# Loads and products of the RWKV-7 scan in another order: keys, queries, values

## The chip, the cores and the metric

The kernel runs on one core of a Trainium2 chip. The metric is the device time of one launch in microseconds. The engines are PE (matmul), PEld (its weight load), DVE, ACT, POOL and SP; SP issues nearly all transfers. A step's matmuls in float32 appear in the trace as two rows for each product of the code.

## What is computed

Two layers over 512 latent and 256 context tokens of width 1024. Layer 0 is a hybrid of attention and a gated linear recurrence. Layer 1 is a bidirectional RWKV-7 mixer, and its scan is the stage of the change:

```python
def wkv_scan(r, w, kk, bvec, k, v, s0, reverse):
    def step(s, inp):
        r_t, w_t, kk_t, b_t, k_t, v_t = inp
        sk = jnp.einsum('bhvk,bhk->bhv', s, kk_t)
        s = s * w_t[:, :, None, :] - sk[..., None] * b_t[:, :, None, :] + v_t[..., None] * k_t[:, :, None, :]
        return s, jnp.einsum('bhvk,bhk->bhv', s, r_t)
    ...
    s_fin, y = lax.scan(step, s0, xs, reverse=reverse)

def rwkv7_mixer(...):
    ...
    for d, rev in enumerate((False, True)):
        s_c, y_c = wkv_scan(rc, dc[d][0], kkc, dc[d][1], dc[d][2], vc, s0, rev)
        _, y_l = wkv_scan(rl, dl[d][0], kkl, dl[d][1], dl[d][2], vl, s_c, rev)
```

## The kernel before

The scan is done in chunks of 64 tokens, both directions at once: `order` (line 1049) lists 12 steps, four of the context and then eight of the latents, each with a forward and a backward chunk. A step works on eight pairs of heads, `kt` 0 to 7, of 128 channels.

Stages ahead of the scan write to DRAM, chunk by chunk: `kbd` (keys and removal vectors with their decay), `qld` and `qcd` (queries of latents and context), `vd` (values), `ld` (the triangles to be inverted). The scan loads them again.

`tm_feed(i)` (line 1052) prepares step `i`, and is a generator that yields between its parts. Its first part loads: the keys KB (two tiles, for pairs 0 to 3 and 4 to 7, each loaded in two halves), the queries QZ (two halves, into one of two standing tiles), the values W (two halves). Then come four groups of products of QZ and KB, each for two pairs, masked by DVE into G (line 1082), and then two groups that turn KB by PE with the identity (line 1096), which ACT copies into KT. `tm_step(i, kt)` (line 1159) is the scan of one pair: products of G and W, of the inverted triangle XT and rh, the update of W by DVE, products of KT and W into the new state S, and for latents the outputs from W, G, S and QZ. It has 20 products for each pair in a latent step.

`tm_scan` (line 1276) runs both together: after each `tm_step(i, kt)` it takes one part of `tm_feed(i + 1)`. So in the text the loads of step `i + 1` stand behind pair 0 of step `i`, the four groups of products behind pairs 1 to 4, the two groups of turns behind pairs 5 and 6. Between them stand the loads and the inversion of a triangle (`tm_invert`, at pair 0 of every second step), the two parts of `tm_below` (pairs 2 and 4), and from step 9 on the group norm of finished chunks (`tm_post`, at pair 2), which loads bo.

Buffers set what may run when. KB has two tiles, W two, QZ two standing ones: the queries of step `i + 1` go where step `i - 1` read its own. The products, the turns, `tm_below` and the z of `tm_post` share the two PSUM tiles mm2.

The text's order is not the order of the queues. The program is written under `tile.TileContext(nc, schedule_with_timeline_sim=True)` (line 1522): a planner lays out each engine's queue in advance, taking at each moment what its plan holds to be ready, and of several ready ones the one that stands first in the text. On the chip each queue then runs in the order laid out.

Of the kernel before, what the change touches and what calls it, by code (L numbers as in the profile page):

```python
# [7 lines left out]
F32 = mybir.dt.float32  # L8
# [7 lines left out]
P = 128  # L16
D = 1024
KT = 8
# [16 lines left out]
class Net:  # L35
# [457 lines left out]
    def recurrence(self, i, ps, gw, m):  # L493
# [3 lines left out]
        rgv = lambda n, i: self.rgv[:, RGV[n], i:i + 1]  # L497
        W = 2 + NL + 3 + NC + 1
        xp = self.sb([P, W], F32, "rgxp", 1)
        for z0, z1 in ((0, 2), (2 + NL, 5 + NL), (W - 1, W)):  # L500
            nc.gpsimd.memset(xp[:, z0:z1], 0.0)
# [442 lines left out]
    def tm_prep(self, kt, lw):  # L944
# [49 lines left out]
        for d in range(2):  # L994
# [4 lines left out]
            else:  # L999
                (nc.vector if kt == KT - 1 else nc.gpsimd).tensor_mul(X[:, 1], X[:, 1], k)  # L1000
                ek, eq, er = E[1][:, :, 0:64], E[0][:, :, 1:65], E[0][:, :, 0:64]
            nc.gpsimd.tensor_copy(self.dec0[:, kt, d], E[1][:, :, 64])
            KB = self.sb([P, 12, 128], F32, "KB", 3)
            nc.vector.tensor_mul(KB.rearrange("p c (b i) -> p b c i", b=2), X.rearrange("p b (c i) -> p b c i", i=64),
                                 ek.unsqueeze(1).to_broadcast([P, 2, 12, 64]))
            nc.sync.dma_start(self.kbd[d, kt], KB)
            ql, qc = self.sb([P, 8, 128], F32, "ql", 3), self.sb([P, 4, 64], F32, "qc", 3)
# [4 lines left out]
            nc.sync.dma_start(self.qcd[d, kt], qc)  # L1012
            KBs.append(KB)
            qs.append((ql, qc))
# [34 lines left out]
    order = [(c, 19 - c) for c in range(8, 12)] + [(c, 7 - c) for c in range(8)]  # L1049
    half = staticmethod(lambda n: slice(64 * n, 64 * n + 64))  # L1050

    def tm_feed(self, i, KB=None, W=None):

        nc, half = self.nc, self.half
        f = self.feeds[i] = {}
        cs = self.order[i]
        lat = cs[0] < 8
        m = 128 if lat else 64
        KB = KB or [self.sb([P, 4, 2, 128], F32, "KB", 2) for _ in range(2)]
        W = f["W"] = W or self.sb([P, KT, 2, 2, 64], F32, "W", 2)  # L1060
        QZ = f["QZ"] = self.QZ[i % 2]
        by = lambda z: z.rearrange("k (n p) m -> p (k n) m", n=2)
        flat = lambda z: z.rearrange("p k n m -> p (k n) m")
        for d in range(2):
            h = half(1 - d)
            for g in range(2):
                nc.sync.dma_start(flat(KB[g][h]), by(self.kbd[d, 4 * g:4 * g + 4, :, cs[d]]))
            nc.sync.dma_start(flat(QZ[h, :, :, d, 0:m]), by(self.qld[d, :, :, cs[d]] if lat else self.qcd[d, :, :, cs[d] - 8]))
        for d in range(2):
            v = self.vd[64 * cs[d]:64 * cs[d] + 64].rearrange("t (k n v) -> t k n v", n=2, v=64)  # L1070
            nc.sync.dma_start(W[half(d), :, d], v)
        f["G"], f["KT"] = [], []
        yield
        for g in range(4):
            ps = self.mm2()
            for j in range(2):
                for n in range(2):
                    x = 2 * m * (2 * j + n)
                    self.mm(ps[:, x:x + 2 * m], KB[g // 2][:, 2 * (g % 2) + j, n], QZ[:, 2 * g + j, n, :, 0:m], True, True)
            G = self.sb([P, 2, 2, 2, m], F32, "G", 8)  # L1080
            f["G"].append(G)
            nc.vector.tensor_mul(G.rearrange("p k n d t -> p (k n) d t"),  # L1082
                                 ps[:, :8 * m].rearrange("p (k d t) -> p k d t", d=2, t=m),
                                 self.gmask[:, :, 0:m].unsqueeze(1).to_broadcast([P, 4, 2, m]))
            if i:

                for d in range(2):
                    h = half(1 - d)
                    nc.scalar.activation(G[h, :, :, d, 0:64], QZ[h, 2 * g:2 * g + 2, :, d, 0:64], AF.Copy)
            yield  # L1090
        for g in range(2):
            ps = self.mm2()
            for j in range(4):
                for n in range(2):
                    x = 256 * j + 128 * n
                    nc.tensor.transpose(ps[:, x:x + 128], KB[g][:, j, n], self.ident)  # L1096
            T = self.sb([P, 4, 2, 128], F32, "KT", 3, pool=self.gp)
            nc.scalar.activation(T, ps.rearrange("p (k n x) -> p k n x", k=4, n=2), AF.Copy)
            f["KT"].append(T)
            yield  # L1100

    def tm_invert(self, j):
# [56 lines left out]
    def tm_step(self, i, kt):  # L1159
# [4 lines left out]
        g, j = kt // 4, kt % 4  # L1164
        W = f["W"][:, kt]
        XT = self.XT[i // 2][:, i % 2]
        Q = f["QZ"][:, kt]
        G = f["G"][kt // 2][:, kt % 2]
# [107 lines left out]
    def tm_scan(self):  # L1276
        nc, a, half = self.nc, self.a, self.half
        self.gmask = self.sb([P, 2, 128], F32, "gmask")
        nc.sync.dma_start(self.gmask, a["gmask"])
        self.umask = self.sb([P, 2], I32, "umask")  # L1280
        nc.sync.dma_start(self.umask, a["umask"])

        qz = lambda j: self.sb([P, KT, 2, 2, 128], F32, "QZ%d" % j)
        q = qz(0)
        ahead = [self.sb([P, 4, 2, 128], F32, "KB", 2) for _ in range(2)], self.sb([P, KT, 2, 2, 64], F32, "W", 2)
        self.QZ = [q, qz(1)]
        for j, z in enumerate(self.QZ):
            for d in range(2):
                nc.gpsimd.memset(z[half(d), :, :, d], 0.0)  # L1289
        self.feeds, self.S, self.Sd = {}, [None, None], [None, None]  # L1290
        n, below = len(self.order), iter(())
        for _ in self.tm_feed(0, *ahead):
            pass
        for i in range(n):
            feed = self.tm_feed(i + 1) if i + 1 < n else iter(())
            for kt in range(KT):
                self.tm_step(i, kt)
                next(feed, None)
                if i % 2 == 0 and kt == 0 and 0 <= i < n - 4:
                    self.tm_invert(i // 2 + 2)  # L1300
                if i % 2 == 1 and kt == 2 and i + 1 < n:
                    below = self.tm_below(i // 2 + 1)
                if (i % 2 == 1 and kt in (2, 4) or i % 2 == 0 and kt in (2, 4)):
                    next(below, None)
                if i == 1 and kt < 2:
                    src = a["gg"].rearrange("o (k n v) -> o k n v", n=2, v=64)[:, :, kt]
                    nc.sync.dma_start(self.gg[half(kt)], src.to_broadcast([64, KT, 64]))
                if i >= 9 and kt == 2:
                    self.tm_post(i - 5)
                if i == n - 2 and kt == 4:  # L1310
                    self.out1_ahead()
# [216 lines left out]
```

## Time and profile before

| | |
|---|---|
| median of 3 runs | 2261.44 us (2256.51 to 2264.19) |
| profiled execution | 2269.31 us |
| its span | 2267.5 us |
| mean granted clock of PE | 0.942 |
| PE busy | 2023.4 us, 89% |
| DVE busy | 1145.4 us, 51% |
| ACT busy | 869.6 us, 38% |
| POOL busy | 519.6 us, 23% |

The rows below come from the profiled execution. Times count from the start of its span. The scan lies between 1466 and 1820 us. A tile's name before `<-` is what an instruction writes, the names after it are what it reads: `mm<-QZ,KB` are the products, `mm<-ident,KB` the turns, `sc<-...` the scan of the pairs.

### The profile page before, as it was taken

How to read it: one execution, taken by the hardware profiler on the slowest of the kernel's cores; microseconds unless marked ns; L12 is line 12 of the kernel's file. 1: busy time of each engine (PE TensorE's matmuls, PEld its weight loads, DVE VectorE, ACT ScalarE, POOL GpSimd, SP SyncE). 2: the span in 40 equal slices, each digit the busy share in tenths (PEclk: the TensorE clock that was granted, in tenths of full speed). 3: DMA queues.
4: the chain of work that ended last, by engine and by line, in shares of the span. 5: the costliest groups of instructions: out<-in, count | busy, mean ns of one | idle time of the engine just before them, and what ended most of it. 6: DMA issues, size and time to landing. Idle time of an engine off the chain costs nothing. (4 is left out here: it accounts for less than half of the span.)

```text
span 2267.5 us, 37320 instructions
## 1 busy us (share of the span) xinstructions
PE 2023.4 (89%) x15710; PEld 1619.3 (71%) x15710; DVE 1145.4 (51%) x1835; ACT 869.6 (38%) x1333; POOL 519.6 (23%) x530
## 2 busy tenths in 40 slices
PE   5888889999999999997987769779787778999999
PEld 3666547778888888875765449667676666888887
DVE  4556664342222222328647997648575684333333
ACT  3664454231121221317744543346454432232321
POOL 0122331010010100105004983661500220110110
PEclk8999999999999999998998778889898999999999
DMA  7324441123333122212224659396644440222222
GB/s 282 119 86 136 143 164 41 37 94 119 124 129 113 56 64 67 98 42 79 93 88 148 236 223 214 71 143 102 113 91 80 76 140 19 93 93 93 93 93 93
DMA packets 231944, 248.93 MB, mean 110 GB/s; under 512 B 52448, under 2 KB 209504, under 8 KB 225376
## 3 DMA queue, kind: packets, MB, share of 16 engines
q1 hardware_dynamic: 229728, 241.30, 36.8%
q0 software_dynamic: 896, 3.15, 0.4%
q8 instruction: 123, 2.02, 0.4%
q10 hardware_dynamic: 1152, 2.10, 0.2%
q14 instruction: 45, 0.37, 0.1%
HBM read 200.82 MB, written 41.94 MB: 107 GB/s over the span
## 5 line engine op out<-in xcount | busy, mean ns | idle before, releaser
L264 ACT ACTIVATE whi<-wst 128x1024 fp32r<-128x1024 f32 x160 | 169.2, 1059 | 587.3 <-PE mm L47 567.0
L47 PE MATMUL mm<-hhi,whi 128*128 128x512 f32 (+1 forms) x992 | 346.8, 356 | 16.2 <-ACT hhi L250 6.7
L47 PE MATMUL mm<-hlo,whi 128*128 128x512 f32 (+1 forms) x992 | 352.0, 356 | 3.6 <-DVE hlo L251 3.4
L47 PE MATMUL mm<-hhi,wlo 128*128 128x512 f32 (+1 forms) x992 | 349.6, 353 | 0.0
L265 DVE TENSOR_TENSOR wlo<-wst,whi 128x1024 fp32r<-128x1024 f32 x160 | 199.9, 1251 | 255.2 <-ACT whi L264 252.4
L345 POOL TENSOR_TENSOR mp<-mr 128x768 f32<-128x768 f32 (+1 forms) x64 | 109.9, 1719 | 848.1 <-ACT mr L344 848.1
L47 PE MATMUL mm<-ahi,wlo 128*128 128x512 f32 (+1 forms) x704 | 252.9, 359 | 0.0
L47 PE MATMUL mm<-ahi,whi 128*128 128x512 f32 (+1 forms) x704 | 252.9, 360 | 0.0
L47 PE MATMUL mm<-alo,whi 128*128 128x512 f32 (+1 forms) x704 | 252.5, 359 | 0.0
L300 DVE SCALAR_TENSOR_TENSOR Xt<-mm,mod,Xt 128x512 f32<-128x512 f32 (+1 forms) x112 | 70.6, 653 | 336.8 <-PE mm L47 336.6
L47 PEld LDWEIGHTS mm<-hhi,whi 128*128 128x128 f32 x992 | 187.8, 191 | 55.2 <-ACT hhi L250 8.7
L47 PEld LDWEIGHTS mm<-hlo,whi 128*128 128x128 f32 x992 | 188.9, 190 | 32.1 <-DVE hlo L251 6.6
L47 PEld LDWEIGHTS mm<-hhi,wlo 128*128 128x128 f32 x992 | 188.4, 190 | 28.3 <-issue 0.8
L47 PEld LDWEIGHTS mm<-ahi,whi 128*128 128x128 f32 x704 | 132.2, 188 | 28.1 <-issue 6.7
L47 PEld LDWEIGHTS mm<-ahi,wlo 128*128 128x128 f32 x704 | 132.5, 188 | 22.0 <-DVE wlo L265 1.1
L47 PEld LDWEIGHTS mm<-alo,whi 128*128 128x128 f32 x704 | 132.4, 188 | 21.9
L47 PE MATMUL mm<-QZ,KB 128*128 128x256 f32 (+1 forms) x384 | 96.4, 408 | 48.1 <-DMA QZ<-qlr 20.3
L47 PEld LDWEIGHTS mm<-QZ,KB 128*128 128x128 f32 x384 | 74.1, 227 | 60.3 <-issue 26.3
L347 DVE TENSOR_TENSOR alo<-mp,ahi 128x768 fp32r<-128x768 f32 (+1 forms) x64 | 54.9, 858 | 113.1 <-ACT ahi L346 113.0
L1082 DVE TENSOR_TENSOR G<-mm,gmask 128x1024 f32<-128x1024 f32 (+1 forms) x48 | 50.2, 1047 | 88.1 <-PE mm L47 87.8
L346 ACT ACTIVATE ahi<-mp 128x768 fp32r<-128x768 f32 (+1 forms) x64 | 47.3, 739 | 110.3 <-POOL mp L345 110.3
L47 PE MATMUL sc<-W,G 128*64 128x64 f32 (+1 forms) x1280 | 67.8, 233 | 12.8 <-DVE S L1194 10.3
(462 smaller groups left out, 4207.7 us busy)
## 6 DMA issues: line engine op xcount, KB each, us to landing
wst<-in_mlp_w_dram SPq DMA_DIRECT2D x64, 1024.0 KB, 5.4
wst<-in_ada_w_dram SPq DMA_DIRECT2D x48, 1024.0 KB, 6.4
kbr<-KB SPq DMA_DIRECT2D x16, 768.0 KB, 4.5
KB<-kbr SPq DMA_DIRECT2D x48, 256.0 KB, 5.6
wst<-in_rw_w_rkv_dram SPq DMA_DIRECT2D x8, 1024.0 KB, 5.4
qlr<-ql SPq DMA_DIRECT2D x16, 512.0 KB, 3.3
QZ<-qlr SPq DMA_DIRECT2D x16, 512.0 KB, 8.8
wst<-in_hy_w_in_dram SPq DMA_DIRECT2D x7, 1024.0 KB, 5.3
```

The source lines that it names most:

```text
L47: self.nc.tensor.matmul(out, lhsT, rhs, start=start, stop=stop)
L264: nc.scalar.activation(hi, w, AF.Copy)
L265: nc.vector.tensor_sub(lo, w, hi.bitcast(F32))
L300: self.nc.vector.scalar_tensor_tensor(x, ps[:, c0:c1], self.m(l, chunk, v, kt), x, op0=OP.mult, op1=OP.add)
L345: nc.gpsimd.tensor_mul(p[:, :n], r[:, :n], r[:, :n])
L346: nc.scalar.activation(h[:, :n], p[:, :n], AF.Copy)
L347: nc.vector.tensor_sub(o[:, :n], p[:, :n], h[:, :n].bitcast(F32))
L1082: nc.vector.tensor_mul(G.rearrange("p k n d t -> p (k n) d t"), ps[:, :8 * m].rearrange("p (k d t) -> p k d t", d=2, t=m), self.gmask[:, : ...
```

## The change

The loads of the keys become a function of their own, `load_keys(i)`. It is called for step 0 ahead of the scan, and for step `i + 1` at the end of `tm_feed(i)`, behind the second group of turns. `tm_feed` no longer loads keys. It loads the queries first, claims the tile of W behind them and then loads the values. A further `yield` behind the loads puts the four groups of products behind pairs 2 to 5 and the turns behind pairs 6 and 7. The number of loads, products and turns is the same.

```diff
-    def tm_feed(self, i, KB=None, W=None):
+    def load_keys(self, i):
+
+        KB = [self.sb([P, 4, 2, 128], F32, "KB", 2) for _ in range(2)]
+        self.feeds[i] = dict(KB=KB)
+        for d in range(2):
+            for g in range(2):
+                self.nc.sync.dma_start(KB[g][self.half(1 - d)].rearrange("p k n m -> p (k n) m"),
+                                       self.kbd[d, 4 * g:4 * g + 4, :, self.order[i][d]].rearrange("k (n p) m -> p (k n) m", n=2))
+
+    def tm_feed(self, i):
 
         nc, half = self.nc, self.half
-        f = self.feeds[i] = {}
+        f = self.feeds[i]
         cs = self.order[i]
         lat = cs[0] < 8
         m = 128 if lat else 64
-        KB = KB or [self.sb([P, 4, 2, 128], F32, "KB", 2) for _ in range(2)]
-        W = f["W"] = W or self.sb([P, KT, 2, 2, 64], F32, "W", 2)
-        QZ = f["QZ"] = self.QZ[i % 2]
+        KB, QZ = f["KB"], self.QZ[i % 2]
+        f["QZ"] = QZ
         by = lambda z: z.rearrange("k (n p) m -> p (k n) m", n=2)
         flat = lambda z: z.rearrange("p k n m -> p (k n) m")
         for d in range(2):
-            h = half(1 - d)
-            for g in range(2):
-                nc.sync.dma_start(flat(KB[g][h]), by(self.kbd[d, 4 * g:4 * g + 4, :, cs[d]]))
-            nc.sync.dma_start(flat(QZ[h, :, :, d, 0:m]), by(self.qld[d, :, :, cs[d]] if lat else self.qcd[d, :, :, cs[d] - 8]))
+            nc.sync.dma_start(flat(QZ[half(1 - d), :, :, d, 0:m]), by(self.qld[d, :, :, cs[d]] if lat else self.qcd[d, :, :, cs[d] - 8]))
+        W = f.get("W")
+        if i:
+            W = f["W"] = self.sb([P, KT, 2, 2, 64], F32, "W", 2)
         for d in range(2):
             v = self.vd[64 * cs[d]:64 * cs[d] + 64].rearrange("t (k n v) -> t k n v", n=2, v=64)
             nc.sync.dma_start(W[half(d), :, d], v)
+        yield
         f["G"], f["KT"] = [], []
         yield
...
             f["KT"].append(T)
+            if g == 1 and i + 1 < len(self.order):
+                self.load_keys(i + 1)
             yield
```

In `tm_scan` the tiles that were claimed ahead for step 0 become `self.load_keys(0)` and a tile of W in `self.feeds[0]`.

## Rows read from the trace of the kernel before

**Rows 1.** The page's chain that ended last, shares of the span by line.

```profile
PE mm L47 21%; PE sc L47 3%; DMA QZ<-qlr 2%; DMA KB<-kbr 1%; DMA XT<-ldr 1%; PE aux L47 1%; DVE zt L1124 1%; DVE Z L1125 1%; PE mm L1096 1%; DVE G L1082 0%; DVE gn L196 0%; DMA wv<-in_rw_w_rkv_dram 0%; POOL Z L1125 0%; POOL QZ L1289 0%; POOL zt L1124 0%
```

**Rows 2.** Waits of PE, 1466 to 1820: us in total, times, longest.

```profile
PE mm L47 <- DMA QZ<-qlr: 20.3, 4, 7.8
PE mm L47 <- issue: 11.6, 2, 8.1
...
PE mm L47 <- POOL Z L1125: 8.3, 1, 8.3
```

**Rows 3.** Busy time by stretch: step 9's feed, then until step 10's.

```profile
core 0: us, PE busy (x) PEld busy (x) DVE busy (x) ACT busy (x) POOL busy (x), PEclk, DMA share, GB/s
1710.20:1728.80 18.60, 18.59 (x268) 15.21 (x270) 10.07 (x12) 10.27 (x21) 0.00 (x0) 0.84 0.01 3
1728.80:1743.20 14.40, 6.68 (x166) 5.78 (x166) 7.27 (x22) 5.54 (x11) 2.12 (x2) 0.89 1.09 183
```

**Rows 4.** Timeline of PE: start, us, instruction, idle before; step 9's feed, step 10's products.

```profile
1710.21 6.59 PE L47 MATMUL mm<-QZ,KB 128*128 128x256 f32 x16 [5.54 <-DMA QZ<-qlr]
...
1721.96 1.99 PE L47 MATMUL mm<-QZ,KB 128*128 128x256 f32 x8
...
1726.39 1.09 PE L1096 MATMUL mm<-ident,KB 128*128 128x128 f32 x8
...
1743.28 5.43 PE L47 MATMUL mm<-QZ,KB 128*128 128x256 f32 x16 [7.80 <-DMA QZ<-qlr]
```

**Rows 5.** Timeline of SP: the loads for step 10.

```profile
1727.52 2.61 SPq L1067 DMA_DIRECT2D KB<-kbr  x4
1731.12 0.52 SPq L1071 DMA_DIRECT2D W<-vdr  x1
1731.73 1.74 SPq L1068 DMA_DIRECT2D QZ<-qlr  x2
```

**Rows 6.** Timeline of PE and SP: a turn for step 7, loads for step 8.

```profile
1657.70 1.70 PE L1096 MATMUL mm<-ident,KB 128*128 128x128 f32 x8 [0.77 <-DVE G L1082]
...
1659.42 3.60 SPq L1067 DMA_DIRECT2D KB<-kbr  x4
1663.16 1.29 SPq L1068 DMA_DIRECT2D QZ<-qlr  x2
```

**Rows 7.** Timeline of PE: first products for step 8, first part of `tm_below`.

```profile
1674.11 5.86 PE L47 MATMUL mm<-QZ,KB 128*128 128x256 f32 x16 [5.98 <-DMA QZ<-qlr]
...
1680.75 1.20 PE L47 MATMUL mm<-XN,XT 32*32 32x32 f32 x64
```

**Rows 8.** Groups of PE instructions, 1726.3 to 1743.2: count, busy us, mean ns.

```profile
L47 PE MATMUL sc<-rh,XT 64*64 64x64 f32 x48 | 3.0, 231 | 0.0
```

**Rows 9.** Timeline of DVE: XN is made for the `tm_below` of rows 7.

```profile
1651.77 2.09 DVE L1133 STREAM_TRANSPOSE XN<-Z 128x1024 f32<-128x1024 f32 x1
```

**Rows 10.** Timeline of PE in the stage ahead, which uses mm2 too.

```profile
1222.22 0.29 PE L47 MATMUL mm<-ql,KB 64*64 64x64 f32 x2 [1.50 <-DVE KB L1004]
1222.44 1.52 PE L47 MATMUL mm<-ident,rho 128*64 128x128 f32 x22
```

**Rows 11.** Timeline of SP and PE: keys and products for step 1.

```profile
1474.96 0.53 SPq L1233 DMA_DIRECT2D bo<-vdr  x1
...
1478.20 2.85 SPq L1067 DMA_DIRECT2D KB<-kbr  x4
...
1485.29 3.75 PE L47 MATMUL mm<-QZ,KB 128*128 128x128 f32 x16 [8.30 <-POOL Z L1125]
```

**Rows 12.** Timeline of SP and PE: keys and products for step 11.

```profile
1767.64 3.06 SPq L1067 DMA_DIRECT2D KB<-kbr  x2
...
1778.28 3.75 PE L47 MATMUL mm<-QZ,KB 128*128 128x256 f32 x8 [8.10 <-issue]
```

**Rows 13.** The loads of QZ for step 10, by line and stretch.

```profile
DMA to landing us min/median/max: 9.3/10.1/10.8
```

More of the change, by code (lines that the diff above doesn't have):

```diff
@@ L1284, in tm_scan @@
         q = qz(0)
-        ahead = [self.sb([P, 4, 2, 128], F32, "KB", 2) for _ in range(2)], self.sb([P, KT, 2, 2, 64], F32, "W", 2)
+        self.feeds, self.S, self.Sd = {}, [None, None], [None, None]
+        self.load_keys(0)
+        self.feeds[0]["W"] = self.sb([P, KT, 2, 2, 64], F32, "W", 2)
         self.QZ = [q, qz(1)]
@@ L1289, in tm_scan @@
                 nc.gpsimd.memset(z[half(d), :, :, d], 0.0)
-        self.feeds, self.S, self.Sd = {}, [None, None], [None, None]
         n, below = len(self.order), iter(())
-        for _ in self.tm_feed(0, *ahead):
+        for _ in self.tm_feed(0):
             pass
```

## Prediction

> **What bounds the kernel now.** The change touches only the scan of layer 1, so the page comes first, to see whether that stage is bound as the rest is. PE is the busiest engine of the whole span, but the chain of work that ended last also waits for transfers, and by line the first of them are QZ<-qlr 2%, KB<-kbr 1% and XT<-ldr 1% of the span [rows 1]. These are the loads of the scan. Next, the waits of PE inside the scan alone, 1466 to 1820 us: 20.3 us for QZ, 11.6 us that the view calls "issue" (8.1 of it at once) and 8.3 us put down to a POOL operation [rows 2]. Both of these waits of 8 us stand ahead of products whose keys were issued only 7.1 and 10.6 us before [rows 11, 12], so they too are waits for loads.
>
> Then the busy time by stretch, which is the view that decides [rows 3]. The stretches alternate. From the first product of a feed to its last turn (a feed is what `tm_feed` prepares for the next step: four groups of products QZ x KB, then two groups of turns of KB on PE) PE is busy 18.59 of 18.60 us, and the DMA share is 0.01. From there to the next feed's first product it is the other way round: PE 6.68 of 14.40 us, DMA share 1.09. The feed stands for its neighbours. So a step of the latent half (order 4 to 11) is a PE phase followed by a DMA phase, and the two hardly overlap. The reason is in the buffers: KB has two tiles for the two halves of the heads, so the next keys cannot be loaded before the turns have read these, and the turns stand last in the feed. A step shortens if either phase does.
>
> **The change, part by part.** The profiled execution took 2269.31 us with a span of 2267.5, so 1.8 us lie around the span; it lies 7.9 us over the median of the three runs, 2261.44. All terms below are differences inside that span, and I carry them to the median unchanged.
>
> *Keys.* The text moves the four KB loads from the start of the next step to right behind the second group of turns. In the trace they are there already. The order within a queue is the planner's, and the text is only its priority: the turns of the first half end at 1726.39 + 1.09 = 1727.48 and the first KB load is issued at 1727.52 [rows 4, 5]; two steps earlier 1657.70 + 1.70 = 1659.40 and 1659.42 [rows 6]. It is so in seven feeds, those of steps 4 to 10 (two stand). All four loads are out 2.61 us later [rows 5]. Nothing is left to gain: 0 us for the latent feeds. The four SP issues per step are the same number; of what they pass on SP (XT, bo and W loads), only bo matters, in the last feed.
>
> *Queries ahead of values.* QZ stood ahead of W in the text before too (only the W tile was claimed earlier). In the trace one half of W goes out first all the same, at 1731.12 against 1731.73 [rows 5], because SP is free and W's buffer is free a moment sooner. In the feed of [rows 6] SP was still issuing keys, and QZ went first, at 1663.16, right behind the keys [rows 6]. That gives the price: first KB issue to first product is 1743.28 - 1727.52 = 15.8 us with half of W ahead [rows 4, 5], and 1674.11 - 1659.42 = 14.7 us without [rows 6, 7]. So 1.1 us per feed where the order turns round. W leads in five feeds (those of steps 6, 7, 9, 10 and 11; one stands). Bounds: 0 to 5 x 1.1 = 5.5 us gained. I take two of the five, -2.2 us: with the turns later in priority the key issues come closer to the step's end, as in [rows 6], but not in every step.
>
> *Products one pair of heads later.* They come behind the second pair of the step instead of behind the first in priority. But in the trace they start when the queries have landed, not when the text allows it: between the turns of one feed and the products of the next PE had run 48 matmuls rh x XT [rows 8]. A pair has four such products in the code, each two matmul rows here, so six of eight pairs, long past the first or second. The place in the text does not bind: 0. What hides it is the DMA phase; if it bound, one pair is 20 products, 40 matmuls, 6.68 us x 40/166 = 1.6 us by [rows 3], either way.
>
> *Turns one pair later.* They follow from the shift, and KB's release with them. Here the old place is close to binding: the turns stand among the last pair's work (scan matmuls make up the whole 6.68 us behind them [rows 3]). If all of a pair's work slips ahead of the turns, it moves from the DMA phase, where it is hidden, into the PE phase: +1.6 us in each of the seven latent feeds, at most 11 us. Because the products move by the same pair, a pair leaves the PE phase at its front, if they do. The row nearest to the new state is the present one, where turns run in the gaps of a waiting last pair; I take 0, bounds -1.6 and +1.6 per feed.
>
> *The shared PSUM buffers.* Products, turns, the two parts of `tm_below` and the z of `tm_post` share the two mm2 tiles. They are handed out in the order of the text: XN of one inversion is ready at 1651.77 + 2.09 = 1653.86, PE idles 5.98 us before 1674.11, yet the products with XN run only at 1680.75, behind two product groups [rows 7, 9]. An earlier stage shows that a tile waits for the first instruction of the one ahead of it: rho's products, needing nothing new, start 0.22 us behind the first ql x KB product [rows 10]. So `tm_below`, now ahead of the second product group and not behind it, still can't run before the queries land. It changes places inside the PE phase with 1.20 us of work: 0. Bounds: 1.20 us gained per feed if it could fill the wait, nothing lost. In steps 9 and 10 z can start one group sooner: 0 to 1.99 us gained in each [rows 4].
>
> *First and last feed.* The longest single waits are 8.30 us at 1485.29 [rows 11] and 8.10 us at 1778.28 [rows 12]. In the first the KB loads stand behind a bo load, which SP issues at 1474.96 [rows 11], 3.2 us before KB: SP had already taken up bo, and a higher priority of KB does not call it back. In the last, the first two KB loads go out at 1767.64 [rows 12], behind QZ and W and with bo loads around them, since the turns that free KB share PE and mm2 with the group norm there. I take 0 for both; up to 8 us each could go if the keys got ahead of bo.
>
> Sum: 0 - 2.2 + 0 + 0 + 0 + 0 = -2.2 us, 2261.4 - 2.2 = 2259 us. Late next, where a wait shrinks, is the same QZ load again, since it is DMA that works through that phase.
>
> *Two rules beside this.* QZ takes 9.3 to 10.8 us from issue to landing in this phase [rows 13]. The Trainium skill, DMA: Bandwidth & Descriptors (Anatomy of one DMA), puts a transfer (there one that GpSimd issues) at about 2.0 us plus its bytes over 436 GB/s, an estimate of 3.2 us for half of QZ; by it the queries would land about when PE runs out of work, and the waits that the whole sum is about would not exist. The rows are about three times longer, so they decide, and the rule gets no chance of its own. The same skill, Perfetto Trace Analysis (Optimization Strategy), reads a gap that repeats through a stretch as a sign that the next tile has no room; by it neither order nor priority helps here, only a third KB tile. [Rows 3] fit that.
>
> **The rivals.** *Faster.* The reordering does turn queries ahead of half of W in all five feeds (5.5 us), the norm's z starts sooner in two steps (2 to 4 us; 3 taken), and the last feed's keys get ahead of some bo loads (up to 8 us; 4 taken). For: SP was busy with keys in [rows 6] and there the order did turn. Further, a shorter wait returns more than its length: the first sixteen products after a wait took 6.59 us [rows 4] against 2 x 1.99 for two later groups [rows 4], at a mean granted clock of 0.84 in that phase [rows 3]. Against: the release of KB, not its priority, sets the start. 5.5 + 3 + 4 = 12 us, 2249 us; at its best 18 us, 2243.
>
> *Slower.* The turns fall behind the whole of another pair, while the products, which wait for data, start where they start now. Each step's PE phase grows by 1.6 us, keys are issued that much later, and since DMA is full in its phase the queries land that much later too. It decides as soon as the last pair's state updates can run before the turns in the new order. 7 x 1.6 = 11 us, 2272 us. For: scan matmuls stand right behind the turns [rows 3, 8]. Against: they wait for ACT and DVE between their own parts, and turns fill such gaps.
>
> *It does not do what it says.* That the loads come no earlier is not a rival but the core of the forecast: in seven feeds they already go out within 0.1 us of the release.
>
> **How the numbers follow.** A measurement of this kernel can tell about 0.3%, 6.8 us, from no change. Forecast (-2.2, own range -6.8 to +6.8): 0.42. Faster rival: 0.33. Slower rival: 0.25. The predicted time is the forecast's, 2259 us. The range goes from 2244, near the best of the faster case, to 2272, the slower one's sum.
>
> **What would show it.** Right: KB issued within 0.1 us of the turns' end as now; DMA share over 1 between a feed's last turn and the next first product; the wait ahead of products still 4 to 8 us in the feeds of steps 8 to 10; in some feeds QZ issued ahead of both W loads and first KB issue to first product near 14.7 us there. Wrong towards faster: the 8.10 us wait of the last feed gone, or `tm_below`'s products inside a wait. Wrong towards slower: PE phases of over 19.5 us with more scan matmuls ahead of the turns. What would make the whole argument wrong is a planner that, given the new priorities, lays out the queues of the scan altogether differently: the two waits of over 8 us show that single places in SP's order are worth more than all that I priced.

## The result, and the profile after

| | before | changed |
|---|---|---|
| median | 2262.82 us (2256.51 to 2265.15, 4 runs) | 2277.57 us (2275.04 to 2279.84, 4 runs) |
| ratio to before | | 1.0069, 95% interval 1.0046 to 1.0093 |
| profiled execution, its span | 2269.31 us, 2267.5 | 2275.04 us, 2273.3 |

The change makes the kernel 0.69% slower, 14.8 us by the medians. The forecast was 2259 us, in a range that ended at 2272.

The profiled execution of before is a long one for its kernel (2269.31 against a median of 2262.82). For comparing traces I therefore take a second profile as the yardstick: the run with the queries first (experiment 4). Its instructions stand in the same order on PE, DVE, ACT and POOL as in the kernel before, its median is 2262.65 us and its span 2261.9. It is called "the reference" below.

First the waits of PE in the scan of the changed kernel (what waited, what for: us in total, times, longest):

```profile
PE mm L47 <- DMA KB<-kbr: 22.6, 6, 8.6
PE mm L47 <- DMA QZ<-qlr: 14.1, 2, 7.3
PE mm L47 <- issue: 12.2, 2, 6.3
PE mm L47 <- DMA W<-vdr: 4.9, 1, 4.9
PE sc L47 <- DVE W L1193: 4.8, 4, 3.7
PE sc L47 <- DVE S L1205: 4.8, 4, 1.8
```

And three lines of the same view of the kernel before that [rows 2] leave out:

```profile
PE sc L47 <- DVE S L1194: 10.3, 7, 4.5
PE mm L47 <- DMA KB<-kbr: 6.8, 4, 2.8
PE sc L47 <- DVE W L1182: 3.1, 5, 1.0
```

The waits ahead of the products (`PE mm`) change names, and they grow: these lines add up to 53.8 us, with [rows 2] to 47.0 before. Ahead of the products for steps 6 and 7 stand 6.3 and 5.9 us, where the reference has 2.7 and 1.8; ahead of those for step 11 stand 3.8 for 8.0. The scan's own products (`PE sc`) wait less for DVE than before, 9.6 us for 13.4. New among these is only one wait of 3.7 us for an update of W, where the longest was 1.0. Then the two phases of a step, as in [rows 3], for the same feed:

```profile
core 0: us, PE busy (x) PEld busy (x) DVE busy (x) ACT busy (x) POOL busy (x), PEclk, DMA share, GB/s
1716.80:1735.60 18.80, 18.79 (x298) 15.31 (x299) 11.59 (x17) 12.35 (x25) 1.06 (x1) 0.89 0.07 19
1735.60:1748.95 13.35, 5.87 (x151) 5.08 (x150) 5.84 (x18) 3.09 (x8) 1.06 (x1) 0.85 1.16 173
```

They are 18.80 and 13.35 us long, where they were 18.60 and 14.40: the alternation of PE and DMA is as it was, and this step in the middle of the scan is not where the time went. Two other places stand out. The first is the end of step 4. Timeline of DVE in the changed kernel, and PE's wait there (start, us, instruction, idle before):

```profile
1589.09 0.55 DVE L1135 TENSOR_TENSOR zt<-Z 128x30 f32<-128x30 f32 x1
1589.68 0.61 DVE L1136 TENSOR_TENSOR Z<-Z,zt 128x30 f32<-128x30 f32 x1
1590.32 2.04 DVE L1144 STREAM_TRANSPOSE XN<-Z 128x1024 f32<-128x1024 f32 x1
1592.23 1.92 DVE L1145 STREAM_TRANSPOSE XD<-Z 128x1024 f32<-128x1024 f32 x1
1594.00 1.08 DVE L1193 COPY_PREDICATED W<-umask,sc 128x256 f32<-128x256 int32 x3
...
1594.49 0.49 PE L47 MATMUL sc<-W,KT 128*64 128x64 f32 x8 [3.66 <-DVE W L1193]
...
1606.50 3.75 PE L47 MATMUL mm<-QZ,KB 128*128 128x256 f32 x8 [6.30 <-issue]
```

and the same instructions in the kernel before:

```profile
1600.29 0.19 DVE L1125 TENSOR_TENSOR Z<-Z,zt 128x30 f32<-128x30 f32 x1
1600.51 2.07 DVE L1133 STREAM_TRANSPOSE XN<-Z 128x1024 f32<-128x1024 f32 x1
1602.49 1.87 DVE L1134 STREAM_TRANSPOSE XD<-Z 128x1024 f32<-128x1024 f32 x1
```

`tm_below` begins with two transposes on DVE, XN and XD. Before, they came when step 5 had updated W for four of its pairs. Now they come 5.3 us earlier, counted from the scan's first product of QZ and KB (131.5 us behind it, 136.8 before, 135.1 in the reference), and stand ahead of the update of W for step 4's last pair. That update follows XN and XD in DVE's queue, so PE waits 3.66 us for it, and step 4 ends late. The queries for step 6 go into the tile that step 4 reads to its end, so they are late too (the 6.30 us ahead of the products), and the first eight products then take 3.75 us. In the reference sixteen take 3.69 us there, behind a wait of 2.70; in the profile of before sixteen take 6.39, behind 3.48, so slow first products are not new. PE's granted clock is lower in the changed kernel: it is at the lower of its two levels (1.2 GHz) for some 13 of the 25 us below, first from 1594.8 to 1598.1, right behind the wait of 3.66 us, and again from 1605.1, in the wait ahead of the products; in the reference for some 3 us. Busy time of 25 us, from 131.2 us behind the scan's first product, changed kernel and then the reference (columns as above; PEclk is the granted clock; the profile of before has 0.86 in that stretch):

```profile
1590.00:1615.00 25.00, 15.04 (x258) 12.92 (x255) 9.78 (x19) 8.67 (x19) 18.32 (x30) 0.73 0.38 65
```

```profile
1595.17:1620.17 25.00, 22.30 (x408) 18.79 (x406) 15.40 (x33) 15.01 (x33) 19.63 (x33) 0.95 0.35 62
```

The second place is the end of the scan. PE and POOL in the changed kernel:

```profile
1816.93 0.41 PE L47 MATMUL sc<-S,QZ 128*64 128x64 f32 x8
...
1819.78 2.35 POOL L1263 TENSOR_TENSOR Y<-Y,gg 128x1024 f32<-128x1024 f32 x1 [22.35 <-DVE Y L1262]
1822.20 2.88 POOL L1264 TENSOR_TENSOR Y<-Y,bo 128x1024 f32<-128x1024 f32 x1
...
1825.14 3.68 PE L47 MATMUL mm<-ident,Y 64*64 64x64 f32 x64 [7.80 <-POOL Y L1264]
```

and in the kernel before:

```profile
1812.53 2.36 POOL L1252 TENSOR_TENSOR Y<-Y,gg 128x1024 f32<-128x1024 f32 x1 [4.62 <-DVE Y L1251]
1814.97 2.35 POOL L1253 TENSOR_TENSOR Y<-Y,bo 128x1024 f32<-128x1024 f32 x1
...
1816.06 0.40 PE L47 MATMUL sc<-S,QZ 128*64 128x64 f32 x8
1817.37 2.08 PE L47 MATMUL mm<-ident,Y 64*64 64x64 f32 x64 [0.91 <-POOL Y L1253]
```

These are the rows that step 10 completes: the group norm (`tm_post`) takes them through DVE and POOL before PE turns them. Before, PE waited 0.91 us for that chain behind the last step; now it waits 7.80 us. The chain itself is about as long as it was, 16.85 us from step 10's end to the turn, 15.71 in the reference; but step 10 ends 17.5 us later than there and step 11 only 11.8, so less of the chain is hidden.

Laid out against the reference, with both traces set to zero at their first product of QZ and KB (1458.83 and 1464.0):

| up to | changed minus reference, us | of it new |
|---|---|---|
| end of the turns for step 5 | +2.4 | +2.4 |
| step 4's last read of QZ | +9.9 | +7.5 |
| step 5's | +13.7 | +3.8 |
| step 9's | +15.2 | +1.5 |
| step 10's | +17.5 | +2.3 |
| step 11's | +11.8 | -5.7 |
| start of the last turn of Y in the scan's tail | +18.7 | +6.9 |

The 6.9 is 7.80 - 0.91. Against the profile of before itself the same rows are +0.7, +8.3, +8.7, +9.2, +11.5, +5.8 and +12.7 us, although its instructions stand in the same order as the reference's. So the 7.5 at the end of step 4 and the 6.9 in the tail hold against either yardstick; the 3.8 at step 5's end does not. Of the 18.7 us, 5.2 are not seen in the span, since this execution of the changed kernel came to the scan 5.2 us sooner (1464.0 - 1458.83), in a part of the program that the change leaves alone; the rest behind the tail is -2.1, and 18.7 - 5.2 - 2.1 = 11.4 is the difference of the spans, 2273.3 - 2261.9. The medians of the changed kernel and the kernel before say 14.8. So a single profile places the loss, but sizes it only to a few us.

### The profile page after: what moved, and what is told of

It is laid out like the page before. It is cut to its first block, busy times and chain, and to the rows that moved or that the text cites. A ratio compares the mean times of both kernels' runs of the same rounds, so it can differ in the third digit from the quotient of the medians.

```text
span 2273.3 us, 37311 instructions
## 1 busy us (share of the span) xinstructions
PE 2024.9 (89%) x15710; PEld 1622.7 (71%) x15710; DVE 1143.3 (50%) x1835; ACT 867.8 (38%) x1333; POOL 520.8 (23%) x530
## 5 line engine op out<-in xcount | busy, mean ns | idle before, releaser
L47 PE MATMUL sc<-W,G 128*64 128x64 f32 (+1 forms) x1280 | 67.7, 235 | 10.4 <-DVE S L1205 4.8
```

The lines of the kernel that those rows point to most:

```text
L47: self.nc.tensor.matmul(out, lhsT, rhs, start=start, stop=stop)
```

## Experiments

Ratios are to runs of the kernel before taken beside each kernel; 0.1% is 2.3 us. "Step 4 ends" is step 4's last read of QZ, "tail" the start of the last turn of Y in the scan's tail, both behind the scan's first product, from each run's own profile; "norm" is PE's wait ahead of that turn.

| kernel | ratio, 95% interval | step 4 ends | tail | norm |
|---|---|---|---|---|
| before, its own profile | 1 | 130.4 | 353.6 | 0.9 |
| changed | 1.0069 (1.0046 to 1.0093) | 138.7 | 366.3 | 7.8 |
| 1 second yield alone | 1.0068 (1.0054 to 1.0082) | 137.8 | 362.0 | 7.8 |
| 2 loads moved alone | 0.9995 (0.9984 to 1.0006) | 126.3 | 345.8 | 0.9 |
| 3 keys early alone | 0.9995 (0.9985 to 1.0005) | 130.4 | 350.0 | 0.9 |
| 4 queries first alone (reference) | 0.9990 (0.9980 to 1.0000) | 128.7 | 347.6 | 0.9 |
| 5 turns later alone | 1.0046 (1.0031 to 1.0061) | 133.4 | 359.2 | 6.5 |
| 6 products later alone | 1.0032 (1.0018 to 1.0046) | 137.2 | 354.6 | 2.4 |
| 7 last feed alone | 1.0018 (1.0007 to 1.0030) | 128.9 | 351.8 | 6.2 |
| 8 all feeds but the last | 1.0054 (1.0036 to 1.0072) | 138.3 | 363.4 | 2.0 |
| 9 inversion on POOL, else before | 1.0041 (1.0025 to 1.0057) | 132.1 | 361.3 | 6.4 |
| 10 the same with the yield | 1.0022 (1.0009 to 1.0036) | 135.4 | 355.4 | 2.4 |
| 11 yield, `tm_below` and norm later | 1.0018 (1.0008 to 1.0029) | 131.8 | 351.1 | 2.9 |
| 12 yield, `tm_below` later | 1.0003 (0.9991 to 1.0014) | 130.3 | 347.5 | 5.2 |
| 13 yield, norm later | 1.0037 (1.0022 to 1.0052) | 138.1 | 359.7 | 5.2 |
| 14 changed, `tm_below` and norm later | 1.0016 (1.0005 to 1.0028) | 130.5 | 353.9 | 2.9 |
| 15 products one pair earlier | 0.9984 (0.9972 to 0.9996) | 127.4 | 346.6 | 0.0 |
| 16 the same, turns between products | 0.9951 (0.9937 to 0.9964) | 117.4 | 328.4 | 2.6 |
| 17 queries in halves | 0.9977 (0.9962 to 0.9992) | 133.0 | 346.7 | 6.6 |
| 18 the two before together | 0.9899 (0.9881 to 0.9916) | 121.9 | 332.0 | 6.4 |

The kernel before and experiment 4 have one order of instructions, and their marks differ by 1.7 us at the end of step 4 and by 6.0 in the tail: marks that differ by no more are not told apart here.

### Which part of the change costs

Experiment 1, the kernel before with the second yield alone:

```diff
             nc.sync.dma_start(W[half(d), :, d], v)
+        yield
         f["G"], f["KT"] = [], []
```

> The kernel before with the second yield alone: products and turns one pair of heads later, loads as they were. Theory (the shift costs: the turns fall behind a whole pair, and the step ahead ends later): it carries the loss, 2274 to 2280 us against 2262.8. Rival (the loss comes from the loads' new places): within 4 us of the kernel before, 2259 to 2267. Rival (neither: each edit lays the engines' queues out anew, and the loss is one place in them): anything, with the loss not where the changed kernel has it.

Experiment 2, the changed kernel without that yield:

> The changed kernel without the second yield: keys loaded behind the turns, queries ahead of values, but products and turns behind the pairs where they stood before. Theory (the shift costs): within 4 us of the kernel before, 2259 to 2267. Rival (the loads' places): 2274 to 2280. If this and the run with the shift alone each cost about half, the parts add up and neither theory stands alone.

Experiment 3, only the keys moved (experiment 2 with the W tile claimed ahead of the queries, as before):

> The kernel before with one edit: the four loads of the keys stand behind the turns of the feed ahead. The prediction: 0 us, 2262.8 +- 3, since they go out within 0.1 us of the turns' end anyway. Rival (the place of the keys against bo, XT and W costs): over 2268; the other way (keys get ahead of bo in the first or the last feed): 2255 or less, with one of the two waits of 8 us gone.

Experiment 4, the kernel before with one line moved:

```diff
-        W = f["W"] = W or self.sb([P, KT, 2, 2, 64], F32, "W", 2)
...
+        W = f["W"] = W or self.sb([P, KT, 2, 2, 64], F32, "W", 2)
         for d in range(2):
             v = self.vd[64 * cs[d]:64 * cs[d] + 64].rearrange("t (k n v) -> t k n v", n=2, v=64)
```

> The kernel before with one edit: the W tile is claimed behind the loads of the queries. By the prediction's price of 1.1 us for each feed where the order of W and QZ turns round: -2 us if it turns in two feeds, -5.5 if in all five, 2257 to 2261. Rival (the order of these two loads is set by when their buffers come free, so nothing turns): 2262.8 +- 2. If queries ahead lose: over 2266.

Measured: +0.68% for the yield, and -0.05%, -0.05% and -0.10% for the moved loads, none of them apart from no change. The yield carries the whole loss, the loads nothing. In experiment 4 SP still sends half of W ahead of the queries, as in [rows 5]:

```profile
1721.97 2.61 SPq L1066 DMA_DIRECT2D KB<-kbr  x4
1725.57 0.52 SPq L1071 DMA_DIRECT2D W<-vdr  x1
1726.18 1.61 SPq L1067 DMA_DIRECT2D QZ<-qlr  x2
```

The order of text does not turn the two loads round: W's buffer comes free a moment sooner, and SP is idle then. It is so in the same five feeds.

### Turns or products, last feed or the others

Experiment 5, a yield between products and turns (turns behind pairs 6 and 7, products where they were):

```diff
             yield
+        yield
         for g in range(2):
             ps = self.mm2()
```

> The kernel before with a yield between products and turns: the turns stand one pair later, the products where they stood. This is the prediction's slower rival done by itself (turns fall behind a whole pair, keys go out later). Theory A (the later turns carry the loss inside the scan): +6 to +11 us against the kernel before, with keys issued at or behind the last reads of the queries, not 4 to 5 us ahead of them, and the stretch from those reads to the next products some 2 us longer in the steps 7 to 9. Rival B (the later products carry it): within 3 us of the kernel before.

Experiment 6, the second yield, and no yield behind the last group of products:

```diff
+        yield
         f["G"], f["KT"] = [], []
...
-            yield
+            if g < 3:
+                yield
         for g in range(2):
             ps = self.mm2()
```

> The kernel before with the products one pair later and the turns where they stood (the fourth product group and the first turns come behind the same pair). Theory A (turns carry it): within 3 us of the kernel before inside the scan. Rival B (products carry it: the first part of tm_below and the norm's z come ahead of the second product group, and the step ahead ends later): +6 to +15, with the gap from the first to the second products over 5 us as in the changed kernel (3.5 in the kernel before).

Experiments 7 and 8, the second yield under `if i == 11:` and under `if i < 11:`:

> The kernel before with the second yield in the last feed alone. Theory C (half of the loss is the end: the last feed's later products let the step ahead end later, and the group norm of its rows, which stood hidden behind the last step, now ends 7 us behind it): +5 to +8 us, with the wait for the norm's rows (POOL, Y) near 7.8 us instead of 0.9. Rival D (the end is late only because the whole scan is laid out anew): within 2 us.

> The kernel before with the second yield in all feeds but the last. Theory C: the other half, +5 to +9 us, with the wait for the norm's rows behind the last step near 0.9 us as in the kernel before. Rival D: all of it, +13 to +17. If this and the run with the last feed alone add up to the whole (15 to 17), the two are separate.

Measured: turns +0.46% and products +0.32%, together 0.78 against 0.68 for both at once; last feed +0.18% and the others +0.54%, together 0.72. Both splits add up within their intervals. Theory A (turns alone) and rival B (products alone) are both half right. B's mark is there: from the first to the second group of products it takes 5.8 to 8.1 us in the feeds of steps 5 to 11. A's marks are mostly absent: the keys are issued 3.8 and 4.1 us ahead of the last reads of the queries in steps 7 and 8, behind them in steps 6 and 9, and the stretch from those reads to the next products is 14.1, 11.4 and 13.5 us in steps 7 to 9, in the reference 13.6, 11.7 and 15.3. So the size of A came true without its path. Theory C has the places right: the last feed alone costs from step 10 on, and PE's wait for the norm shows it,

```profile
1813.86 3.34 PE L47 MATMUL mm<-ident,Y 64*64 64x64 f32 x64 [6.19 <-POOL Y L1255]
```

with the ends of steps 4 and 9 at 128.9 and 294.7 (reference 128.7 and 293.2), and all the others cost inside the scan, with the norm's wait at 2.0. In size it fails on both sides: the last feed costs 4.1 us, not 5 to 8, and all the others 12.2, above C's 5 to 9 and just under rival D's 13 to 17.

### Is it the order on DVE

In every run with the products later and `tm_below` and its inversion left as they were (1, 6, 8, 13 and the changed kernel) XN and XD stand ahead of step 4's last updates, and step 4 ends at 137 to 139. In none of the others does it end later than 135.4. To take the cause away, the inversion that makes the Z they read goes from DVE to POOL:

```diff
-    pool_inverse = (1, 2, 4)
+    pool_inverse = (1, 2, 3, 4)
```

> Control: the kernel before with the inversion that runs beside steps 2 to 5 (j = 3) on GpSimd, not on VectorE. It takes some 16 us of work off VectorE near the end of step 4. Theory E (VectorE's order at the end of step 4 costs only the shifted kernel, since only there the two transposes of the inverse stand ahead of the step's last updates): within 4 us of the kernel before.

> The same move of the inversion, in the kernel with the second yield alone, which costs 15.4 us against the kernel before. Theory E: the end of step 4 falls back from 12 us behind the turns to about 6, and this kernel is only 7 to 10 us over the control. Rival (the end of step 4 is only where a delay shows that the later products make): still 14 to 17 over the control.

Measured: +0.41% without the yield and +0.22% with it. Theory E wanted the shifted kernel 7 to 10 us over this control and its rival 14 to 17; it is not over the control at all (2268.95 us in the median, the control 2272.41). With the yield, XN and XD now come in the middle of step 4, where the longest wait of PE beside them is 1.25 us:

```profile
1582.76 2.07 DVE L1134 STREAM_TRANSPOSE XN<-Z 128x1024 f32<-128x1024 f32 x1
...
1589.86 2.00 DVE L1135 STREAM_TRANSPOSE XD<-Z 128x1024 f32<-128x1024 f32 x1
...
1601.45 0.78 DVE L1183 COPY_PREDICATED W<-umask,sc 128x256 f32<-128x256 int32 x2
```

and step 4 ends 5.7 us behind the turns ahead of it, as in the reference, instead of 11.9. The turns themselves end 3.9 us later than in experiment 1, so step 4 ends only 2.3 us sooner. In the control it is the other way round: there the transposes moved ahead of step 4's last updates of S, and PE waits for them,

```profile
1585.77 2.09 DVE L1133 STREAM_TRANSPOSE XN<-Z 128x1024 f32<-128x1024 f32 x1
1587.73 1.91 DVE L1134 STREAM_TRANSPOSE XD<-Z 128x1024 f32<-128x1024 f32 x1
1589.51 0.77 DVE L1194 SCALAR_TENSOR_TENSOR S<-sc,dec,Sd 128x64 f32<-128x64 f32 x4
...
1589.96 0.45 PE L47 MATMUL sc<-W,G 128*64 128x64 f32 x8 [2.91 <-DVE S L1194]
```

the same distance grew from 5.7 to 10.0, and the norm's wait to 6.4 us, without any shift. So theory E's claim that the order hurts only the shifted kernel falls. That a wait of this kind arises in the control too is shown; that it carries the control's 0.41% is not, since step 4 ends at 132.1 there, 1.7 us behind the profile of before, and experiment 5 has a like tail (359.2, with a wait of 6.5) with the transposes in their old place.

### Moving the neighbours along

Experiment 11 moves `tm_below` and the norm one pair later with the yield, 12 only `tm_below`, 13 only the norm, 14 both in the changed kernel:

```diff
-                if i % 2 == 1 and kt == 2 and i + 1 < n:
+                if i % 2 == 1 and kt == 3 and i + 1 < n:
                     below = self.tm_below(i // 2 + 1)
-                if (i % 2 == 1 and kt in (2, 4) or i % 2 == 0 and kt in (2, 4)):
+                if kt in (3, 5):
                     next(below, None)
...
-                if i >= 9 and kt == 2:
+                if i >= 9 and kt == 3:
                     self.tm_post(i - 5)
```

> The second yield, and with it the two parts of tm_below and the norm (tm_post) one pair later too, so that the tiles of mm2 are handed out in the order of the kernel before and only the pairs of the scan stand elsewhere. Theory O (the order among the users of mm2, with tm_below and z now ahead of the second product group, carries the loss): within 4 us of the kernel before. Rival S (what costs is that products and turns stand behind one more pair of the step): +11 to +18.

> The second yield, and tm_below one pair later with it; the norm stays. Theory E (the two transposes of the inverse stand ahead of step 4's last updates because tm_below kept its place while the products moved): the end of step 4 is again about 6 us behind the turns, the POOL wait behind the last step stays at 6 to 8 us, total +6 to +10 us over the kernel before (15.4 without this edit). Rival (the norm's place carries what was regained): still +13 to +16.

> The second yield, and the norm (tm_post) one pair later with it; tm_below stays. Theory E: step 4 still ends 12 us behind its turns; if the order of z and the second product group makes the norm late, the POOL wait falls from 7.8 to under 3 us and the total is +8 to +11. If the norm's lateness only follows from the late end of step 10, the wait stays and the total is +14 to +16.

> The changed kernel as it is, with tm_below and the norm one pair later too. Theory (order among the users of mm2, not the shift): +2 to +6 us over the kernel before, as the second yield alone with these edits (+4.1), since the loads' new places cost nothing. Rival (the loads' places cost something beside the shift): over +8.

Measured: with `tm_below` moved along, the loss of 0.68% is gone (0.03%, -0.09 to +0.14). On DVE, XN is behind a pair of step 5 again:

```profile
1598.79 0.43 DVE L1183 COPY_PREDICATED W<-umask,sc 128x256 f32<-128x256 int32 x1
1599.12 2.07 DVE L1134 STREAM_TRANSPOSE XN<-Z 128x1024 f32<-128x1024 f32 x1
1601.06 1.92 DVE L1135 STREAM_TRANSPOSE XD<-Z 128x1024 f32<-128x1024 f32 x1
```

Step 4 ends at 130.3. The norm's wait is still 5.2 us, near the 6 to 8 of theory E, but step 11 ends 4.5 us sooner than in the reference (342.3 against 346.7), so the tail starts where it did; theory E had left 6 to 10 us. Neither case of experiment 12's expectation came true: the result lies under theory E's. The norm alone takes back 0.31%, and step 4 still ends at 138.1; its total of 8.4 us is that of the case with the wait under 3 us, but the wait is 5.2. The two edits do not add: 0.65% and 0.31% apart, 0.50% together, which leaves 0.18% (4.1 us, at the edge of theory O's 4). In the changed kernel both together take back 0.53 of 0.69%, and the 3.6 us left are inside the 2 to 6 expected. So most of the loss goes when `tm_below` keeps its place against products and turns, and the loads have no part in it. What is left of the shift then is nothing measurable in experiment 12 and 0.18% in 11, where the norm keeps its place too. Moving `tm_below` moves its transposes, its products on PE and its claims on mm2 at once; no run moved the transposes alone. Nor does this explain experiment 5, which lost 0.46% with `tm_below` where it was against the products.

### The other direction, and what sets the start of the products

Experiment 15 drops the only yield ahead of the products (products behind pairs 0 to 3, turns behind 4 and 5). Experiment 16 is 15 with the turns of the first half of the heads between the second and the third group of products:

```diff
-        f["G"], f["KT"] = [], []
-        yield
-        for g in range(4):
+        f["G"], f["KT"] = [], []
+        for e in range(2):
+            for g in (2 * e, 2 * e + 1):
...
-        for g in range(2):
+            for g in (e,):
```

> The kernel before without the yield behind the loads: products and turns one pair of heads earlier, the opposite of the change. Rival S (the place behind the pairs costs 15 us a pair): faster by 4 us or more. The prediction's step on the products (their place in the text does not bind, six of eight pairs are done by then): within 3 us. Theory O: the norm's z and tm_below now come one product group later, +-5 us.

> The kernel with products one pair earlier (3.6 us faster than before), and the first turns between the second and the third product group, so that half of KB comes free two product groups sooner. Theory (the wait ahead of the products is one for the queries, whose tile comes free only at the end of the step): within 3 us of that kernel, 2257 to 2262. Rival (the keys' release sets it, as the prediction had it): 3 to 8 us faster than that kernel, under 2256.

Experiment 17 is the kernel before with keys and queries loaded by halves of the heads, 18 is 16 with the same:

```diff
-            for g in range(2):
-                nc.sync.dma_start(flat(KB[g][h]), by(self.kbd[d, 4 * g:4 * g + 4, :, cs[d]]))
-            nc.sync.dma_start(flat(QZ[h, :, :, d, 0:m]), ...)
+        for g in range(2):
+            ks = slice(4 * g, 4 * g + 4)
+            for d in range(2):
+                h = half(1 - d)
+                nc.sync.dma_start(flat(KB[g][h]), by(self.kbd[d, ks, :, cs[d]]))
+                nc.sync.dma_start(flat(QZ[h, ks, :, d, 0:m]), ...)
```

> The kernel before with the queries loaded in two halves of four pairs each (four loads of 256 KB for two of 512 KB), keys and queries of a half together. If the release of the queries' tile at the step's end sets the products' start: the first half goes out some 8 us ahead of the step's end, the waits ahead of the products fall from 4 to 8 us to under 3, and the kernel is 10 to 30 us faster. If the keys' release sets it (two KB tiles, turned last): within 4 us of the kernel before.

> Products one pair earlier, the first turns between the second and third product group (11 us faster than before), and the queries in halves. If both releases count: the first half of keys and queries can both be loaded while PE works, and it is a further 8 us or more faster, under 2246. If only the keys' release did: within 4 us of 2253.6.

Measured: 15 is 0.16% faster, 16 0.49%, 17 0.23%, 18 1.01% (2242.57 us in the median, 21 us under before). For 15 the rival's "4 us or more" and the prediction's "within 3" stand on both sides of 3.6. In 16 the keys of the first half come free two product groups sooner and it shows, 0.33% more: there the keys' release counts, as the rival had it and against the theory: the first keys for steps 9 and 11 are issued 15 us ahead of the queries. 17 falls between its two cases. Together the two releases bring more than the sum of their parts, 1.01 against 0.49 + 0.23, by a little more than the intervals allow. The loads of 18 show why:

```profile
1672.11 1.25 SPq L1068 DMA_DIRECT2D KB<-kbr  x2
1674.12 1.25 SPq L1069 DMA_DIRECT2D QZ<-qlr  x2
...
1692.02 0.52 SPq L1072 DMA_DIRECT2D W<-vdr  x1
1692.63 1.26 SPq L1069 DMA_DIRECT2D QZ<-qlr  x2
1693.94 0.62 SPq L1072 DMA_DIRECT2D W<-vdr  x1
1694.66 1.26 SPq L1068 DMA_DIRECT2D KB<-kbr  x2
```

The first halves of keys and queries go out 18 to 20 us ahead of the values, which wait for the step's end, so half of the keys and queries no longer share the stretch behind the step's end. The wait ahead of these products is still 4.70 us, and the norm's wait in the tail 6.45, so more is left there.

## Why the prediction was wrong, step by step

*What bounds the kernel* held: two phases a step, hardly overlapping, and the buffers behind them. Experiments 16 and 18 gained where loads went out ahead of the step's end.

*Keys, 0 us* held: -0.05% alone. In the changed kernel the first turns for step 9 end at 1731.74 + 1.09 = 1732.83 and KB is issued at 1732.87.

*Queries ahead, -2.2 us from two of five feeds* failed in its mechanism: alone, they turn in no feed, and the measured -0.10% reaches to zero. In the changed kernel W still leads in four of those five feeds. The price of 1.1 us for a feed was never put to the test.

*Products one pair later, 0 us* failed: 7.2 us alone (0.32% of 2264). The argument was that the products wait for data, so that their place in the text does not bind. It was read from the feed of step 10 alone, where six pairs were done. In the feed of step 5 no pair of step 4 stood ahead of the first products, and two do now: there the place binds. And the text also ranks the products against everything that shares DVE and mm2 with them: behind the first group for step 9 PE now ran `tm_below` and parts of the scan's pairs,

```profile
1716.81 3.78 PE L47 MATMUL mm<-QZ,KB 128*128 128x256 f32 x8 [4.87 <-DMA W<-vdr]
1720.52 1.40 PE L47 MATMUL mm<-XN,XT 32*32 32x32 f32 x64
...
1722.94 2.43 PE L47 MATMUL mm<-QZ,KB 128*128 128x256 f32 x10
```

where [rows 4] have sixteen products in one go.

*Turns one pair later, 0 with bounds of 1.6 us a feed, at most 11* was sized well as a bound and not as a value: 10.4 us alone (0.46%), but not as 1.6 in each of seven feeds. By the profile of experiment 5 the scan is 4.7 us behind the reference at the end of step 4, 6.4 at the end of step 9 and 11.6 in the tail. Of the 4.7, 3.2 stand already at the first products for step 5. What makes the loss, with XN in its old place, stays open.

*The shared PSUM buffers* is the step that failed worst. It counted the 1.20 us that `tm_below` takes on PE, found that they only change places inside the PE phase, and wrote "nothing lost". It left out that `tm_below` starts with two transposes on DVE, although [rows 9] show one of them, 2.09 us long. In the changed kernel and in experiments 1, 6, 8 and 13 they stand ahead of step 4's last update of W, and PE waits 3.25 to 3.66 us for it there; no other run has such a wait for W at that place. Experiment 12 shows what the place of `tm_below` against products and turns was worth in all: 0.65%, 14.7 us. How much of that the two transposes carry, and how much the rest of `tm_below`, no run separates. The Trainium skill, PSUM — Partial Sum Buffer (Engine vs sequencer instructions), says that the queues of ScalarE, VectorE and GpSimd are strictly first in, first out; the trace agrees: W's update starts at 1594.00, behind XN and XD, and PE is idle for 3.66 us ahead of 1594.49.

*First and last feed, 0 us* was half right: the wait of 8.30 us is 8.63 now, and that of 8.10 us [rows 12] shrank to 3.81. The faster rival had priced that at 4 us, and what it gained was given back at once: the norm behind the last step became the latest.

*The rivals.* The slower one had the sign, and 2272 of the measured 2277.6 us, with a chance of 0.25; its place (the PE phase of each latent step) is not where the time went, see the phases above. The range ended with its sum alone, and products and turns were never both counted as lost, though the two of them alone measure 7.2 and 10.4 us. The last sentence of the prediction, that a new layout of all queues would overturn it, named the danger, and had no chance or price of its own.

*The two rules.* The repeating gap that the Trainium skill, Perfetto Trace Analysis (Optimization Strategy), reads as a possible sign of too little room for the next tile was there, and experiments 16 and 18 agree, in that earlier room brought time. My conclusion from it, that only a third KB tile would help, was too narrow (no run has a third tile): experiment 18 makes the room by freeing halves earlier, with the same tiles, and gains 21 us.

What stays open: how much of the loss the transposes on DVE carry; why the turns alone cost 0.46%, which `tm_below` in its new place takes back as well; why the norm alone, moved later, takes back 0.31% with step 4 as late as before; and why the two edits together gain less than `tm_below` alone. Each run is a new layout of all queues, and its last few us are not traced to single places.

## What to carry to other kernels

Where a planner lays the queues out from the text's order, a part that is moved changes its rank against every neighbour on every engine that it or they use: list all first instructions of the parts that it now stands behind or ahead of, the small ones on DVE above all, and move those along that belong to it. What stands ahead of a step's last update on an engine that is only half busy can still cost about its whole length there (3.66 us of wait behind 3.96 of transposes), if the next loads wait for that step's end. And where PE and DMA take turns, look which read frees each buffer last; freeing the keys earlier brought 0.33% (16 against 15), halving the queries' loads 0.23%, and both together 0.85% (18 against 15).

## What was not expected

DVE was busy 50% of the span and yet held up the end of step 4: with two transposes of 2.04 and 1.92 us ahead of the last update of W the step ended 7.5 us later behind its turns, 3.66 of them one wait of PE, and PE's granted clock was 0.73 in the 25 us around it (0.95 in the reference). The control with the inversion on POOL lost 0.41% though it took work off DVE, the fuller of the two engines (DVE 50%, POOL 23% of the span in the changed kernel).
